# Making keys and queries behind the tiles of channels in a bidirectional encoder block: one phase's matmuls moved into another

## The chip, the cores and the metric

The kernel runs on one core of one Trainium2 chip. The metric is the device time of one execution in microseconds (us). The engines are PE (TensorE, matmuls), DVE (VectorE), ACT (ScalarE), POOL (GpSimd) and SP (SyncE), which issues most of the DMAs.

## The reference, cut

One layer of an encoder runs on a sample of 2048 rows and, with the same weights, on a prompt of 256 rows (`s` below); `D_MODEL` is 1024, there are 8 heads, a key has 64 plain and 32 rotary elements, a value has 64.

```python
def _layer(x, norm_pre, w_in, conv_w, q_norm, w_uq, kv_norm, w_ukv, w_out, norm_post):
    hdn = _rmsnorm(x, norm_pre)
    proj = jnp.einsum('bsd,de->bse', hdn, w_in)
    u, b_gate, c_gate, z_conv, q_lat, kv_lat, k_pe, z_attn = jnp.split(proj, _split_points(), axis=-1)
    conv_out = b_gate * _short_conv(c_gate * u, conv_w) * jax.nn.silu(z_conv)
    q = jnp.einsum('bsr,re->bse', _rmsnorm(q_lat, q_norm), w_uq).reshape(b, s, N_HEADS, QK_NOPE_DIM + QK_ROPE_DIM)
    q_nope, q_pe = jnp.split(q, [QK_NOPE_DIM], axis=-1)
    q_pe = _apply_rope(q_pe, cos[:, None, :], sin[:, None, :])
    kv = jnp.einsum('bsr,re->bse', _rmsnorm(kv_lat, kv_norm), w_ukv).reshape(b, s, N_HEADS, QK_NOPE_DIM + V_HEAD_DIM)
    k_nope, v = jnp.split(kv, [QK_NOPE_DIM], axis=-1)
    k_pe = _apply_rope(k_pe, cos, sin)
    ...
    attn_out = _attention(q_full, k_full, v) * jax.nn.silu(z_attn)
    mix = jnp.concatenate([conv_out, attn_out], axis=-1)
    out = jnp.einsum('bse,ed->bsd', mix, w_out)
    return x + _rmsnorm(out, norm_post)
```

## The kernel before, in words

The rows stand as T = 2304 columns, the sample's 2048 first and the prompt's 256 last. Every operand of a projection is kept as a high and a low part, and `mm3` (L87) multiplies high by high (L91), high by low (L92) and low by high (L93) into one PSUM tile: three matmuls for each term.

**Phase 1** (`phase1`, L103) goes over the rows in two halves `hf` of 1152. In each half it makes the latents of nine tiles of rows (`latents` L176, `turn_latents` L213: query latents of 384, key and value latents of 256 and the 32 rotary columns, stored to DRAM as `lat_s` and `kpe_s`), then goes through 20 tiles of 128 channels, `etile` (L242; 40 in both halves, counted by `n`). For each of three chunks `ci` of 384 rows `etile` issues 24 matmuls (8 terms) into a PSUM tile `o` of the tag `mm`, which has six buffers; DVE, ACT and POOL evacuate it as the kind of channel wants (`u`, gates, SiLU, and behind each fourth tile the short convolution `conv`, L295). The weights of a tile come through a staging buffer and are split into `whi` and `wlo` (`load_w`, L231). In the last four tiles of a half the chunks become the attention's gate `za`, which SP stores to `gate_s` (L256 to L258).

The opening of phase 2 is a generator, `Phase2.open` (L405). It loads the weights of the up-projections (uq, uk, uv) through two staging buffers, squares them (L436) for norms that scale them, sums these on PE (`w_ssq` L451, `rot_sum` L462, `all_sum` L484), turns the result into row scales, splits the weights into f16 high and low parts and rotates the key's 32 rotary columns into `kr_s`. `phase1` starts it behind tile 23 and takes two of its steps behind each tile from there.

**Phase 2** (`Phase2.run`, L559) works on nine chunks of 256 rows; chunk 0 is the prompt. `keys` (24 matmuls, a chunk's four tiles of 128 channels in one wide PSUM tile), `values` (12 matmuls of 512 columns in two halves) and `queries` (54 matmuls, two of six tiles rotary) come in the order k0 v0 q0, k1 v1 ... k8 v8, q1 ... q8. Keys and queries are evacuated chunk by chunk to f16 high and low parts and stored to DRAM (`kn_s`, `qn_s` on ACT's queue, `qr_s` on SP's). The attention loads them from there: `load_k` (five DMAs), `load_q_of` (nine DMAs), `load_kc` (two DMAs, the low parts of the rotary keys). For the prompt these are one `load_k` and two `load_q_of`; for the sample, `k_0` holds two heads over all 2048 rows and `q_0` two heads over 512.

Before a block's softmax the kernel takes the maximum of its scores: `max_chunks` (L733), for the prompt 8 steps `m_p`, for block 0 of the sample 32 steps `m_0`, each a matmul of 512 columns (L752) and a DVE reduction (L753). `max_columns` and `max_rows` (L756, L768) fold the maxima into the queries. `prompt` (L833) is the whole attention for a pair of the prompt's heads: scores `sp`, ACT's exponents `pp`, POOL's sum `accp`, the product with the values `op`, and `finish` (L811) with `rp` and the division. `tile_encoder` (L974) drives all that: it takes one step of a generator at a time behind each tile that `run` yields, the prompt's steps (`sides["p"]`) behind k3 and later, the rest of them at q1, and block 0's maxima (`sides[0]`) behind the query tiles q3 to q8. From the first key tile on PE, DVE, ACT and POOL run in the order in which the program says it (`manual_schedule`); in phase 1, and on SP throughout, the framework's scheduler sets the order.

Then follow the **attention** of the sample (`steps` L861, `values` L911, with the first product of weights and values at L920) and **phase 4**, the output projection. The change leaves both as they are.

Of the kernel before, what the change touches and what calls it, by code (L numbers as in the profile page):

```python
# [21 lines left out]
P = 128  # L22
# [80 lines left out]
def phase1(g, x, x_t, w_e, w_lat, npre, convw, open_phase2):  # L103

    nc, tc = g.nc, g.tc
    with ExitStack() as ctx:
# [135 lines left out]
        def etile(n):  # L242
# [3 lines left out]
            for ci in range(3):  # L246
# [84 lines left out]

        n = 0
        for hf in range(2):
# [24 lines left out]
            for j in range(5):  # L358
                if j < 4:
                    edge(hf, j, True)  # L360
                for e in range(4):
# [3 lines left out]
                    etile(n)  # L365
# [23 lines left out]
class Phase2:  # L389
# [15 lines left out]
    def open(self, w_uq, w_uk, w_uv, w_lat, npre, qg, kvg, pst, ps):  # L405
# [4 lines left out]

        g, nc, tc = self.g, self.g.nc, self.g.tc
# [30 lines left out]
        yield  # L442
# [15 lines left out]
        yield  # L458
# [22 lines left out]
        yield  # L481
# [16 lines left out]
        yield  # L498
# [9 lines left out]
        yield  # L508
        for m in range(0, 12, 3):
# [3 lines left out]
            if m % 2:  # L513
                yield

        for name, src, kt, n, at in srcs[1:] + srcs[:1]:
            hi, lo = self.ws[name]
            for k in range(kt):
# [4 lines left out]
                yield  # L523

        for a, b in ((0, 768), (768, 1536), (1536, TS), (TS, T)):
# [5 lines left out]
            yield  # L531
# [7 lines left out]
            yield  # L539
        for what in ("kv", "q"):  # L540
            self.load(0, pw, what)
        tmp.close()


    def load(self, ci, pb, what):

        g, nc = self.g, self.g.nc
        at, n = self.chunks[ci]
        a, num = (3, 2) if what == "kv" else (0, 3)
        lt = pb.tile([P, n // P, 2, num, P], F16, tag=f"lt_{what}", bufs=1 if ci == 0 else 4 if what == "kv" else 2, name=f"lt_{what}{ci}")  # L550
# [3 lines left out]
        if what == "q":  # L554
            tb = pb.tile([P, 2, CB], F32, tag="tb", bufs=1 if ci == 0 else 2, name=f"tb{ci}")
            nc.sync.dma_start(tb[:, :, :n], self.table[:, :, at % TS : at % TS + n])
        self.lt[what, ci] = lt, tb

    def run(self, pv):  # L559

        g, ws = self.g, self.ws
        nc, tc = g.nc, g.tc
        with ExitStack() as ctx:
            pb = ctx.enter_context(tc.tile_pool(name="p2b", bufs=2, reuse_waits="tile"))

            def rope(dst, src, tb, name):

                t = pb.tile([P, 2, CB], F32, tag="rs", bufs=2, name=f"rs_{name}")[:, :, : src.shape[2]]
                cos, sin = (tb[:, w : w + 1, : src.shape[2]].to_broadcast(list(src.shape)) for w in range(2))
                nc.vector.stream_shuffle(t, src, SWAP)  # L570
                nc.vector.tensor_tensor(dst, src, cos, op=ALU.mult)
                nc.gpsimd.tensor_tensor(t, t, sin, op=ALU.mult)
                nc.gpsimd.tensor_tensor(dst, dst, t, op=ALU.add)

            late = []

            def store(queue, dst, src, tok):

                queue.dma_start(dst[:, :, tok].rearrange("w (m p) t -> p w m t", p=P), src)

            def block(name, n):
                return pb.tile([P, 2 * 4 * CB], F16, tag="s4", bufs=3, name=name)[:, : 8 * n].rearrange("p (w m t) -> p w m t", w=2, m=4)

            def wide(name, m, n):
                return g.wide(name)[:, : m * n].rearrange("p (m t) -> p m t", m=m)

            def keys(ci):
                at, n = self.chunks[ci]
                lt, _ = self.lt["kv", ci]
                sk = block(f"sk{ci}", n)  # L590
                hi, lo = ws["uk"]
                o = wide(f"k{ci}", 4, n)
                for m in range(4):
                    msl = slice(m * P, (m + 1) * P)
                    mm3(nc, o[:, m], [(hi[:, k, msl], lo[:, k, msl], lt[:, :, 0, k], lt[:, :, 1, k]) for k in range(2)])
                    if m == 3:
                        split(nc, sk[:, 0], sk[:, 1], o, BACK)
                        late.append(lambda: store(nc.scalar, g.kn, sk, slice(at, at + n)))
                    yield "k", ci, m

            def values(ci):
                at, n = self.chunks[ci]
                lt, _ = self.lt["kv", ci]
                hi, lo = ws["uv"]
                o = wide(f"v{ci}", n // P, H * DV)
                for m in range(n // P):
                    mm3(nc, o[:, m], [(lt[:, m, 0, k], lt[:, m, 1, k], hi[:, k, :], lo[:, k, :]) for k in range(2)])
                    if m == n // P - 1:
                        nc.scalar.activation(pv[:, at // P : (at + n) // P], o, AF.Copy, scale=BACK)
                        while late:  # L610
                            late.pop(0)()
                    yield "v", ci, m

            def queries(ci):
                at, n = self.chunks[ci]
                tok = slice(at, at + n)
                lt, tb = self.lt["q", ci]
                sqr = pb.tile([P, 2, CB], F32, tag="sqr", bufs=1, name=f"sqr{ci}")[:, :, :n]
                sqp = pb.tile([P, 2, 2, CB], F16, tag="sqp", bufs=1, name=f"sqp{ci}")[:, :, :, :n]
                sq = block(f"sq{ci}", n)  # L620
                hi, lo = ws["uq"]
                r = g.narrow(f"qr{ci}", "o")[:, : 2 * n].rearrange("p (m t) -> p m t", m=2)
                o = wide(f"q{ci}", 4, n)
                for m in (4, 5, 0, 1, 2, 3):
                    msl = slice(m * P, (m + 1) * P)
                    mm3(nc, o[:, m] if m < 4 else r[:, m - 4], [(hi[:, k, msl], lo[:, k, msl], lt[:, :, 0, k], lt[:, :, 1, k]) for k in range(3)])
                    if m == 5:
                        rope(sqr, r, tb, f"q{ci}")
                    if m == 3:
                        split(nc, sq[:, 0], sq[:, 1], o, BACK)  # L630
                        nc.scalar.activation(sqp[:, 0], sqr, AF.Copy, scale=BACK)
                        nc.gpsimd.tensor_scalar(sqr, sqr, BACK, None, op0=ALU.mult)
                        nc.gpsimd.tensor_tensor(sqp[:, 1], sqr, sqp[:, 0], op=ALU.subtract)
                        store(nc.scalar, g.qn, sq, tok)
                        store(nc.sync, g.qr, sqp, tok)
                    yield "q", ci, m

            last = len(self.chunks)
            plan = [("kv", 0), ("q", 0)] + [("kv", ci) for ci in range(1, last)] + [("q", ci) for ci in range(1, last)]
            ahead = [(w, ci) for w, ci in plan if ci]  # L640
            for i, (what, ci) in enumerate(plan):
                while ahead and plan.index(ahead[0]) <= i + (3 if ahead[0][0] == "kv" else 1):
                    w, c = ahead.pop(0)
                    self.load(c, pb, w)
                if what == "kv":
                    yield from keys(ci)
                    yield from values(ci)
                else:
                    yield from queries(ci)
# [324 lines left out]
def tile_encoder(ctx, tc, x, x_t, w_e, w_lat, w_uq, w_uk, w_uv, w_out, convw, npre, qg, kvg, npost, table, y):  # L974
# [35 lines left out]
    side = []  # L1010

    def prompt():

# [9 lines left out]
    sides = {"p": prompt(), 0: at.max_chunks(0)}  # L1023
    last = len(p2.chunks) - 1
    for kind, ci, m in p2.run(g.v):
        if (kind, ci, m) == ("k", 0, 0):
            order.enter_context(tc.manual_schedule(engines=engines))
            at.load_kc()
        if (kind, ci, m) == ("q", 0, 3):
            at.load_k("p")  # L1030
            at.load_q("p")

            nc.scalar.activation(at.ps.tile([P, 10], F32, tag="warm", bufs=1, name="warm"), g.mhalf, AF.Exp)
        if (kind, ci, m) == ("v", last, 1):
            at.load_k(0)
        if (kind, ci, m) == ("q", 2, 3):
            at.load_q(0)
        if kind in "kv" and ci > 2:
            next(sides["p"], None)
        if (kind, ci, m) == ("q", 1, 4):  # L1040
            for _ in sides["p"]:
                pass
        if kind == "q" and (ci > 3 or ci == 3 and m in (2, 3)):
            next(sides[0], None)
        if (kind, ci, m) == ("q", 7, 3):
            at.load_q(1)
    for _ in sides[0]:
# [100 lines left out]
```

## Time and profile before

| | |
|---|---|
| Median of 3 runs | 1690.15 us (1689.59 to 1693.16) |
| Profiled execution, its own time | 1692.56 us |
| its span in the trace | 1690.6 us, mean granted clock 0.994 |
| PE busy | 1647.5 us (97%) |
| POOL, DVE, ACT busy | 878.5, 750.2, 581.6 us |
| Phase 1, tiles of channels, second half | 392.5 to 646.1 us of the span |
| Phase 2, prompt and block 0's maxima | 646.1 to 812.9 us |
| Attention of the sample | 812.9 to 1483.9 us |

A row of the timeline or of a group names the line, the operation, its output and inputs, the shape and the duration; what stands in brackets behind a row is the idle time of the engine just ahead of it and the work that ended this. PEclk is the share of TensorE's full clock that was granted in a stretch.

### The profile page before, as it was taken

How to read it: one execution, taken by the hardware profiler on the slowest of the kernel's cores; microseconds unless marked ns; L12 is line 12 of the kernel's file. 1: busy time of each engine (PE TensorE's matmuls, PEld its weight loads, DVE VectorE, ACT ScalarE, POOL GpSimd, SP SyncE). 2: the span in 40 equal slices, each digit the busy share in tenths (PEclk: the TensorE clock that was granted, in tenths of full speed). 3: DMA queues.
4: the chain of work that ended last, by engine and by line, in shares of the span. 5: the costliest groups of instructions: out<-in, count | busy, mean ns of one | idle time of the engine just before them, and what ended most of it. 6: DMA issues, size and time to landing. Idle time of an engine off the chain costs nothing. (4 is left out here: it accounts for less than half of the span.)

```text
span 1690.6 us, 22364 instructions
## 1 busy us (share of the span) xinstructions
PE 1647.5 (97%) x8870; PEld 1115.8 (66%) x8870; DVE 750.2 (44%) x1125; ACT 581.6 (34%) x804; POOL 878.5 (52%) x637
## 2 busy tenths in 40 slices
PE   8999999999999999978999999999999999999998
PEld 8999999999999997556333333333333333378886
DVE  4333332423474222337556665666666666132122
ACT  7521111452222122411444444444444444512211
POOL 3321221033342112145788988989899898942222
PEclk9999999999999999989999999999999999999999
DMA  8921112364324116378011131113111210034443
GB/s 292 273 87 60 52 52 83 112 165 118 114 94 137 55 62 167 106 194 214 13 32 32 44 85 41 44 32 94 31 45 32 69 44 13 26 105 144 149 141 109
DMA packets 141741, 158.97 MB, mean 94 GB/s; under 512 B 33842, under 2 KB 118116, under 8 KB 141636
## 3 DMA queue, kind: packets, MB, share of 16 engines
q1 hardware_dynamic: 122916, 148.11, 29.3%
q10 hardware_dynamic: 18720, 9.44, 1.9%
q8 instruction: 69, 1.13, 0.3%
q14 instruction: 36, 0.29, 0.1%
HBM read 109.72 MB, written 41.89 MB: 90 GB/s over the span
## 5 line engine op out<-in xcount | busy, mean ns | idle before, releaser
L809 POOL TENSOR_TENSOR acc<-acc,p 128x1024 f32<-128x1024 f32 x224 | 527.9, 2357 | 60.6 <-ACT p L799 50.5
L753 DVE TENSOR_REDUCE mx<-m 128x1 f32<-128x512 f32 x512 | 337.7, 691 | 237.2 <-PE m L752 237.1
L799 ACT ACTIVATE p<-s,exps 128x1024 f32<-128x1024 f32 x256 | 271.4, 1111 | 348.2 <-PE s L794 348.2
L91 PE MATMUL o<-hdn_hi,whi 128*128 128x384 f32 x960 | 323.5, 337 | 0.0
L92 PE MATMUL o<-hdn_lo,whi 128*128 128x384 f32 x960 | 322.7, 336 | 0.0
L93 PE MATMUL o<-hdn_hi,wlo 128*128 128x384 f32 x960 | 322.6, 336 | 0.0
L789 PE MATMUL s<-q,k 128*128 128x512 f16 x1024 | 302.7, 381 | 1.0 <-ACT p L799 1.0
L920 PE MATMUL o<-p,v 128*64 128x512 f32 x1024 | 247.7, 605 | 0.0
L789 PEld LDWEIGHTS <-k 128*128 128x128 f16 x1024 | 90.7, 98 | 190.8 <-issue 101.4
L752 PE MATMUL m<-k,q 96*128 96x512 f16 x512 | 195.4, 382 | 14.4 <-DVE mx L753 8.7
L91 PEld LDWEIGHTS o<-hdn_hi,whi 128*128 128x128 f32 x960 | 180.5, 188 | 0.5
L92 PEld LDWEIGHTS o<-hdn_lo,whi 128*128 128x128 f32 x960 | 180.5, 188 | 0.0
L93 PEld LDWEIGHTS o<-hdn_hi,wlo 128*128 128x128 f32 x960 | 180.5, 188 | 0.0
L920 PEld LDWEIGHTS o<-p,v 128*64 128x64 f32 x1024 | 62.2, 136 | 127.5 <-issue 127.0
L959 PE MATMUL out<-wo,o_cut 128*128 128x512 f32 x576 | 140.4, 396 | 0.0
L959 PEld LDWEIGHTS out<-wo,o_cut 128*128 128x128 f32 x576 | 108.0, 188 | 27.7 <-issue 0.8
L948 POOL TENSOR_TENSOR o_cut<-o_raw,o_cut 128x1024 fp32r<-128x1024 f32 x17 | 40.8, 2399 | 118.3 <-ACT o_cut L945 118.3
L279 POOL TENSOR_TENSOR gt<-gt,z 128x384 f32<-128x384 f32 x24 | 28.7, 1197 | 141.1 <-ACT z L278 141.1
L236 ACT ACTIVATE whi<-w 128x1024 fp32r<-128x1024 f32 x40 | 42.2, 1058 | 172.8 <-PE o L92 159.6
L752 PEld LDWEIGHTS <-q 96*128 96x128 f16 x512 | 49.6, 97 | 63.9 <-issue 6.2
L967 DVE TENSOR_TENSOR yt<-out,g_post 128x1024 f32<-128x1024 f32 x18 | 22.0, 1224 | 150.7 <-ACT junko L966 141.7
L271 POOL TENSOR_TENSOR cu<-cu,rb 128x384 f32<-128x384 f32 (+2 forms) x28 | 27.5, 987 | 112.4 <-DVE cu L270 112.4
(230 smaller groups left out, 2016.4 us busy)
## 6 DMA issues: line engine op xcount, KB each, us to landing
w<-in_w_e_dram SPq DMA_DIRECT2D x40, 512.0 KB, 3.5
x<-in_x_dram SPq DMA_DIRECT2D x18, 512.0 KB, 6.8
o_raw<-mix_s SPq DMA_DIRECT2D x18, 512.0 KB, 4.8
o_raw<-in_x_dram SPq DMA_DIRECT2D x18, 512.0 KB, 5.6
out_dram<-yt SPq DMA_DIRECT2D x18, 512.0 KB, 6.2
q<-qn_s SPq DMA_DIRECT2D x64, 128.0 KB, 2.7
xt<-in_x_t_dram SPq DMA_DIRECT2D x5, 1536.0 KB, 8.3
k<-kn_s SPq DMA_DIRECT2D x12, 512.0 KB, 7.1
```

What stands on the lines that cost most here:

```text
L91: nc.tensor.matmul(out, sh, mh, start=first and i == 0, stop=False)
L92: nc.tensor.matmul(out, sh, ml, start=False, stop=False)
L93: nc.tensor.matmul(out, sl, mh, start=False, stop=last and i == n - 1)
L236: nc.scalar.activation(hi, w, AF.Copy)
L752: nc.tensor.matmul(m, q[:DQK, i, 2, b * P : (b + 1) * P], k[:DQK, i, 1, c * 512 : (c + 1) * 512], start=True, stop=True)
L753: nc.vector.reduce_max(mx[:, u, c : c + 1], m, axis=AX.X)
L789: nc.tensor.matmul(o, k[:, ki, x, ks], q[:, qi, x, :], start=x == 0, stop=False)
L799: nc.scalar.activation(p, o, AF.Exp, scale=g.exps[:, 0:1])
L809: nc.gpsimd.tensor_tensor(self.acc[key], self.acc[key], first, op=ALU.add)
L920: nc.tensor.matmul(self.o[n][i * DV : (i + 1) * DV], g.v[:, kt, h * DV : (h + 1) * DV], p[:, i * QB : (i + 1) * QB], start=kt == 0, stop=k ...
L948: eng.tensor_tensor(ml, m, f(mh), op=ALU.subtract)
L959: nc.tensor.matmul(o[:, w], mh[:, k, :], wk[k // 2][:, k % 2, w], start=k == 0 and wk is hi, stop=False)
```

## The change

Keys and queries of all nine chunks move into phase 1. `etile` calls `between` behind each of its three chunks. `between` takes one step of the opening, and where that step yields 2, two more. The opening starts behind tile 21 instead of tile 23 (`n == 22`), its steps come one behind each chunk, and `keys_queries` follows as part of it: 90 tiles of keys and queries, three behind each of the last thirty chunks. Each has a PSUM tile of its own, of the tag `mm` that the chunks use, is evacuated by itself, and all stores go through SP. Phase 2 keeps the values alone; the prompt's attention and block 0's maxima are interleaved with their eighteen halves and with each other in a new way. The loads of keys and queries for the prompt stand right behind phase 1, those of block 0 behind the first two chunks of values. The number of PE's instructions stays 10976.

```diff
-        def etile(n):
+        def etile(n, between):
...
                     nc.sync.dma_start(g.gate[e * P : (e + 1) * P, c * CH : (c + 1) * CH], za)
+                    between()
                     continue
...
                     conv(hf, j, ci)
+                between()
...
+        opening = iter(())
+
+        def between():
+            for _ in range(next(opening, 0)):
+                next(opening, None)
...
-                    etile(n)
+                    etile(n, between)
...
-                    if n == 24:
+                    if n == 22:
                         opening = open_phase2(pb, ps)
-                    if n >= 24:
-                        next(opening, None)
-                        next(opening, None)
...
-        for what in ("kv", "q"):
-            self.load(0, pw, what)
         tmp.close()
+        self.pb = self.ctx.enter_context(tc.tile_pool(name="p2b", bufs=2, side="right", reuse_waits="tile"))
+        yield from self.keys_queries(ps)
+        for ci in range(3):
+            self.load(ci, "kv")
...
+    def keys_queries(self, ps):
...
+        last = len(self.chunks)
+        for ci in range(2):
+            self.load(ci, "kv")
+            self.load(ci, "q")
+        for ci, (at, n) in enumerate(self.chunks):
+            tok = slice(at, at + n)
+            for what, name, kt, ms in (("kv", "k", 2, 4), ("q", "q", 3, 6)):
...
+                for m in range(ms):
+                    msl = slice(m * P, (m + 1) * P)
+                    o = ps.tile([P, CH], F32, tag="mm", bufs=6, name=f"{name}{ci}_{m}")[:, :n]
+                    mm3(nc, o, [(hi[:, k, msl], lo[:, k, msl], lt[:, :, 0, k], lt[:, :, 1, k]) for k in range(kt)])
+                    if m < 4:
+                        split(nc, s[:, 0, m], s[:, 1, m], o, BACK)
+                    else:
+
+                        t, r = (pb.tile([P, CB], F32, tag=tag, name=f"{tag}{ci}_{m}") for tag in ("rs", "sqr"))
+                        nc.vector.stream_shuffle(t, o, SWAP)
+                        nc.vector.tensor_tensor(r, o, tb[:, 0], op=ALU.mult)
+                        nc.gpsimd.tensor_tensor(t, t, tb[:, 1], op=ALU.mult)
+                        nc.gpsimd.tensor_tensor(r, r, t, op=ALU.add)
+                        nc.scalar.activation(sp[:, 0, m - 4], r, AF.Copy, scale=BACK)
+                        nc.vector.scalar_tensor_tensor(sp[:, 1, m - 4], r, BACK, sp[:, 0, m - 4], op0=ALU.mult, op1=ALU.subtract)
+                    if m == 3:
+                        store(g.kn if what == "kv" else g.qn, s, tok)
+                    if m == 5:
+                        store(g.qr, sp, tok)
+                    if m == ms - 1 and ci + 2 < last:
+                        self.load(ci + 2, what)
+                    yield 2
...
+        for ci, (at, n) in enumerate(self.chunks):
+            if ci + 3 < last:
+                self.load(ci + 3, "kv")
...
+            for m in range(2):
+                mm3(nc, o[:, m], [(lt[:, m, 0, k], lt[:, m, 1, k], hi[:, k, :], lo[:, k, :]) for k in range(2)])
+                if m:
+                    nc.scalar.activation(pv[:, at // P : (at + n) // P], o, AF.Copy, scale=BACK)
+                yield ci, m
...
-    sides = {"p": prompt(), 0: at.max_chunks(0)}
...
+    order.enter_context(tc.manual_schedule(engines=engines))
+    at.load_k("p")
+    at.load_q("p")
+    at.load_kc()
+
+    nc.scalar.activation(at.ps.tile([P, 10], F32, tag="warm", bufs=1, name="warm"), g.mhalf, AF.Exp)
+    side = prompt()
+    for ci, m in p2.run(g.v):
+        if (ci, m) == (1, 0):
             at.load_k(0)
-        if (kind, ci, m) == ("q", 2, 3):
             at.load_q(0)
...
+            first = at.max_chunks(0)
+        if ci > 1:
+            next(side, None)
+        if ci > 2:
+            next(first, None)
+            if m:
+                next(side, None)
+    for _ in side:
+        next(first, None)
+        next(first, None)
+    at.load_q(1)
+    for _ in first:
         pass
     at.max_columns(0)
```

The next two pieces show **PE at the first maximum of block 0** (`m_0_0`). Before, it stands among the query tiles of chunk 3:

```order
L93 MATMUL q_6651<-lt_q_6556,uq_lo 128x256
L752 LDWEIGHTS q_6632
L752 MATMUL m_0_0_6703<-k_6474,q_6632 128x512
L91 LDWEIGHTS uq_hi
L91 MATMUL q_6651<-lt_q_6556,uq_hi 128x256
```

With the change it stands behind the third of the prompt's maxima and ahead of the second half of the values of chunk 3:

```order
L719 MATMUL m_p_7077<-k_p,q_p_6964 128x256
L729 LDWEIGHTS q_7024
L729 MATMUL m_0_0_7082<-k_7018,q_7024 128x512
L91 LDWEIGHTS lt_kv_6991
L91 MATMUL v_7070<-uv_hi,lt_kv_6991 128x512
```

So PE reaches its first use of `k_0` and `q_0` after three and a half of nine chunks of values; before, all values and three chunks of queries stood ahead of it. On **SP behind phase 1** the DMAs of `k_0` (`k_6474` before, `k_7018` now) stood among those of the query chunks:

```order
L729 DMA gate_7574<-gate_s 128x512
L556 DMA tb_6559<-in_table_dram 128x2x256
L693 DMA k_6474<-kn_s 64x2x2048
L696 DMA k_6474<-kn_s 64x2x2048
L697 DMA k_6474<-kn_s 64x2x2048
L579 DMA qr_s<-sqp_6486 128x4x256
L552 DMA lt_q_6556<-lat_s 128x2x384 x2
```

Now they stand behind all eighteen DMAs of the prompt's queries, the two of `kc` and two latent loads:

```order
L700 DMA q_p_6974<-qr_s 32x2x256 x2
L660 DMA kc<-kr_s 32x2304 x2
L562 DMA lt_kv_7008<-lat_s 128x2x256 x2
L670 DMA k_7018<-kn_s 64x2x2048
L671 DMA k_7018<-kr_s 32x2x2048
L672 DMA k_7018<-kr_s 32x2x2048
L673 DMA k_7018<-kn_s 64x2x2048
L674 DMA k_7018<-kn_s 64x2x2048
L691 DMA q_7024<-qn_s 64x2x512
L692 DMA q_7024<-qr_s 32x2x512
```

The nine loads of `q_0` follow those of `k_0` with nothing between them. The third place is the **opening on PE**. The sums of the squared weights, `w_ssq`, stood behind the last chunk of tile 23 and `rot_sum` three chunks later:

```order
L92 MATMUL o_2_3915<-hdn_lo_3078,whi_3757 128x384
L93 MATMUL o_2_3915<-hdn_hi_3077,wlo_3758 128x384
L451 LDWEIGHTS uq_sq
L451 MATMUL w_ssq<-short,uq_sq 128x2
L451 LDWEIGHTS uq_sq
```

Now `w_ssq` stands behind the second chunk of tile 22, and `rot_sum` behind the third:

```order
L92 MATMUL o_1_3842<-hdn_lo_2833,whi_3662 128x384
L93 MATMUL o_1_3842<-hdn_hi_2832,wlo_3663 128x384
L458 LDWEIGHTS uq_sq
L458 MATMUL w_ssq<-short,uq_sq 128x2
L458 LDWEIGHTS uq_sq
```

```order
L91 MATMUL o_2_3908<-hdn_hi_3077,whi_3662 128x384
L92 MATMUL o_2_3908<-hdn_lo_3078,whi_3662 128x384
L93 MATMUL o_2_3908<-hdn_hi_3077,wlo_3663 128x384
L469 MATMUL rot_sum<-rot,ones 128x2
L91 MATMUL o_0_3966<-hdn_hi_2414,whi_3757 128x384
```

So the sums come four chunks earlier on PE, and only one chunk lies between the squares' sums and the next step that needs them. The key and query tiles themselves stand on PE from the second chunk of tile 29 on, three tiles behind each chunk; a chunk's matmuls load their weights themselves, those of the f16 tiles have an instruction for it ahead of each.

## Rows read from the trace of the kernel before

**Rows 1.** Windows: us, busy (x) of PE, PEld, DVE, ACT, POOL, PEclk, DMA share, GB/s.

```profile
392.53:646.14 253.61, 252.22 (x1486) 250.94 (x1484) 107.37 (x200) 54.39 (x89) 72.89 (x80) 1.00 0.30 96
646.14:722.59 76.45, 71.91 (x506) 45.24 (x506) 27.89 (x36) 29.75 (x38) 13.18 (x12) 1.00 0.56 152
722.59:798.80 76.21, 59.61 (x466) 46.68 (x465) 38.47 (x62) 12.07 (x16) 38.58 (x30) 0.91 0.83 212
812.91:1483.87 670.96, 667.62 (x3204) 224.44 (x3203) 388.02 (x578) 306.36 (x317) 602.23 (x274) 1.00 0.15 43
```

**Rows 2.** Timeline of PE among the query tiles: start, length, instruction [idle before].

```profile
740.79 0.37 PE L91 MATMUL qr<-lt_q,uq_hi 128*128 128x256 f16 x1 [6.24 <-DMA lt_q<-lat_s]
752.56 0.58 PE L752 MATMUL m<-k,q 96*128 96x512 f16 x1 [5.12 <-DMA q<-qr_s]
```

**Rows 3.** Windows of PE alone: a key chunk's 24 matmuls, a query chunk's.

```profile
646.14:648.75 2.61, 2.61 (x24) 1.00 0.42 127
722.59:728.49 5.90, 5.90 (x56) 1.00 0.36 110
```

**Rows 4.** Timeline of PE in phase 1, from a small matmul to the latents' fp32r ones.

```profile
377.50 0.43 PE L91 MATMUL pq<-wl_hi,hdn_hi 128*128 128x384 f32 x1
377.76 0.34 PE L92 MATMUL pq<-wl_lo,hdn_hi 128*128 128x384 f32 x1
```

**Rows 5.** Timelines of PE, SP and DVE in the opening.

```profile
442.78 0.28 PE L451 MATMUL w_ssq<-short,uq_sq 128*128 128x2 bf16 x5
...
419.90 0.33 SPq L227 DMA_DIRECT2D kpe_s<-kpt  x1
434.38 0.80 SPq L435 DMA_DIRECT2D uks<-in_w_uk_dram  x2
...
447.68 0.16 DVE L456 TENSOR_TENSOR rot<-ssq 128x1 fp32r<-128x1 f32 x1
```

**Rows 6.** Timeline of SP's queue behind phase 1.

```profile
646.67 0.33 SPq L258 DMA_DIRECT2D gate_s<-za  x1
664.96 0.59 SPq L714 DMA_DIRECT2D q_p<-qn_s  x1
675.22 0.90 SPq L723 DMA_DIRECT2D q_p<-qr_s  x2
727.62 0.59 SPq L693 DMA_DIRECT2D k<-kn_s  x1
750.10 0.54 SPq L715 DMA_DIRECT2D q<-qr_s  x1
```

**Rows 7.** Window in which `k_0`'s large loads move, columns as in rows 1.

```profile
733.00:736.00 3.00, 1.55 (x15) 1.14 (x12) 1.05 (x2) 1.02 (x1) 2.54 (x3) 1.00 1.02 219
```

**Rows 8.** The prompt: window of its `mrp` matmuls, and timeline of one pair of heads.

```profile
680.55:682.80 2.25, 1.21 (x18) 1.09 (x16) 1.18 (x1) 1.76 (x5) 0.00 (x0) 1.00 0.89 258
...
708.73 0.27 PE L845 MATMUL sp<-q_p,k_p 128*128 128x256 f16 x1
710.65 0.28 PE L794 MATMUL sp<-q_p,kc 33*128 33x256 f16 x1
712.13 1.08 PE L857 MATMUL op<-pp,v 128*64 128x256 f32 x8 [0.44 <-ACT pp L799]
713.54 0.65 PE L818 MATMUL rp<-accp,ones_f 128*64 128x256 f32 x4 [0.33 <-POOL accp L851]
```

**Rows 9.** Timelines of DVE and PE from the last maxima to the first values.

```profile
801.99 3.09 DVE L753 TENSOR_REDUCE mx<-m 128x1 f32<-128x512 f32 x5
804.53 0.38 PE L776 MATMUL mr<-ident,mst 128*97 128x128 f16 x4 [0.24 <-DVE mx L753]
812.91 0.65 PE L920 MATMUL o<-p,v 128*64 128x512 f32 x2
```

**Rows 10.** Groups by line: DVE's reciprocals of the prompt.

```profile
L823 DVE RECIPROCAL rsump<-rsump 128x128 f32<-128x128 f32 x8 | 7.0, 922 | 10.9 <-ACT rsump L820 10.9
```

**Rows 11.** Waits: engine, line, waited for; us in total, times, longest us.

```profile
ACT cy L309 <- POOL cu L271: 64.6, 16, 7.1
```

More of the change, by code (lines that the diff above doesn't have):

```diff
@@ L441, in open @@
         nc.scalar.activation(wt, wt, AF.Square, accum_out=kp)
-        yield
+        yield 0
         acc = ps.tile([P, 3, P], F32, tag="tl", name="w_ssq")[:, 0, :28]
@@ L480, in open @@
         unpower(nc, g.inv, col)
-        yield
+        yield 0
         acc = ps.tile([P, 3, P], F32, tag="tl", name="all_sum")[:, 0, :2]
@@ L507, in open @@
             nc.vector.tensor_scalar(diag[:, m], g.ident, c, W_UP, op0=ALU.mult, op1=ALU.mult)
-        yield
+        yield 0
         for m in range(0, 12, 3):
@@ L513, in open @@
             if m % 2:
-                yield
+                yield 0
         for name, src, kt, n, at in srcs[1:] + srcs[:1]:
@@ L538, in open, with load @@
             nc.sync.dma_start(g.kr[:, :, a:b].rearrange("w e t -> e w t"), krp)
-            yield
-        for what in ("kv", "q"):
-            self.load(0, pw, what)
+            yield 0
         tmp.close()
-    def load(self, ci, pb, what):
-        g, nc = self.g, self.g.nc
+        self.pb = self.ctx.enter_context(tc.tile_pool(name="p2b", bufs=2, side="right", reuse_waits="tile"))
+        yield from self.keys_queries(ps)
+        for ci in range(3):
+            self.load(ci, "kv")
+    def load(self, ci, what):
+        g, nc, pb = self.g, self.g.nc, self.pb
         at, n = self.chunks[ci]
         a, num = (3, 2) if what == "kv" else (0, 3)
-        lt = pb.tile([P, n // P, 2, num, P], F16, tag=f"lt_{what}", bufs=1 if ci == 0 else 4 if what == "kv" else 2, name=f"lt_{what}{ci}")
+        turn = self.turn = self.turn + 1
+        lt = pb.tile([P, n // P, 2, num, P], F16, tag=f"lt_{what}", bufs=4 if what == "kv" else 2, name=f"lt_{what}{turn}")
         for w in range(2):
@@ L554, in load @@
         if what == "q":
-            tb = pb.tile([P, 2, CB], F32, tag="tb", bufs=1 if ci == 0 else 2, name=f"tb{ci}")
+            tb = pb.tile([P, 2, CB], F32, tag="tb", name=f"tb{ci}")
             nc.sync.dma_start(tb[:, :, :n], self.table[:, :, at % TS : at % TS + n])
         self.lt[what, ci] = lt, tb
-    def run(self, pv):
[L561 to L649, printed above, removed]
@@ new lines, in keys_queries, with store @@
+    def keys_queries(self, ps):
+        g, ws, nc, pb = self.g, self.ws, self.g.nc, self.pb
+        def store(dst, src, tok):
+            nc.sync.dma_start(dst[:, :, tok].rearrange("w (m p) t -> p w m t", p=P), src)
+        last = len(self.chunks)
[5 more added lines that the diff above has]
+            for what, name, kt, ms in (("kv", "k", 2, 4), ("q", "q", 3, 6)):
+                lt, tb = self.lt.pop((what, ci))
+                hi, lo = ws["u" + name]
+                s = pb.tile([P, 2, 4, CB], F16, tag="s4", bufs=3, name=f"s{name}{ci}")
+                if what == "q":
+                    sp = pb.tile([P, 2, 2, CB], F16, tag="sqp", name=f"sqp{ci}")
+                for m in range(ms):
[19 more added lines that the diff above has]
+                    yield 2
@@ new lines, in run @@
+    def run(self, pv):
+        g, nc = self.g, self.g.nc
+        hi, lo = self.ws["uv"]
+        last = len(self.chunks)
+        for ci, (at, n) in enumerate(self.chunks):
+            if ci + 3 < last:
+                self.load(ci + 3, "kv")
+            lt, _ = self.lt.pop(("kv", ci))
+            o = g.wide(f"v{ci}").rearrange("p (m e) -> p m e", m=2)
+            for m in range(2):
[3 more added lines that the diff above has]
+                yield ci, m
@@ L1021, in prompt @@
             yield from at.prompt(j)
-    sides = {"p": prompt(), 0: at.max_chunks(0)}
[L1024 to L1034, printed above, removed]
+    order.enter_context(tc.manual_schedule(engines=engines))
[6 more added lines that the diff above has]
+        if (ci, m) == (1, 0):
             at.load_k(0)
-        if (kind, ci, m) == ("q", 2, 3):
             at.load_q(0)
[L1038 to L1047, printed above, removed]
+            first = at.max_chunks(0)
[10 more added lines that the diff above has]
+    for _ in first:
         pass
```

9 lines of the change are left out of this document (4 added, 5 removed).

## The prediction

> **What bounds the kernel now.** I read the stages first, as windows: by what is PE held in each? In the second half of phase 1 and in the sample's attention PE is busy for 252 of 254 us and 668 of 671 [rows 1]; no cover is wanted there, and work added there costs its full length. Only the stretch between them has slack: 646.1 to 722.6 and 722.6 to 798.8, where PE is busy 71.9 and 59.6 us, the second at a granted clock of 0.91, and on to the first product with the values at 812.9 [rows 1, 9]. Then the timeline of that stretch: the reader should see two waits for a DMA, 6.24 us for a latent load of the queries and 5.12 us for `q_0` [rows 2]. The change takes key and query matmuls out of this stretch and puts them where PE never waits. The question is whether the stretch shrinks by as much as phase 1 grows. So I forecast two instants: E, where phase 1 ends and the values begin (646.1 before), and the start of the sample's values on PE (812.9 before). Behind that nothing changes and PE sets the pace, so the shift of 812.9 is the shift of the whole.
>
> **E: phase 1 grows.** A key chunk's 24 matmuls take 2.61 us, a query chunk's 54 take 5.90 (its window holds 56 entries) [rows 3]. Nine of each are 9 x 8.51 = 76.6 us, at the same pace as before, since they stand in program order between chunks that never wait. There are 30 changes from f16 to the chunks' matmuls. The nearest rows are a small matmul's successor in phase 1: its second matmul starts 0.26 us after it, against 252.2 / 1486 = 0.17 in the long run [rows 4, 1]; 0.07 to 0.09 for each makes 2 us (0 if the load of weights is covered, 4.5 if both directions cost that and more). The matmuls of the tiles stay hidden for evacuation as long as six PSUM buffers bridge it: the 90 tiles add splits on ACT and DVE, which are busy 54 and 107 of 254 us there [rows 1], so I cost them at nothing. That cover is gone where one of them stands behind an instruction that waits, such as ACT's `cy`, which waits for POOL up to 7.1 us [rows 11]; that is a rival below.
>
> By the Trainium skill ("TensorE: Matmul & The Clock Gate", part on LDWEIGHTS) PE pulls weight loads ahead of matmuls in flight, so the changes of type would cost nothing and the sum would be 2 us less; the row with 0.26 us speaks for a small price.
>
> The opening starts two tiles earlier, and its sums are packed closer. On PE `w_ssq` stood behind tile 23; four chunks of 24 matmuls, 4.1 us each at 0.17, are 16.4 us, so it is reached at 442.8 - 16.4 = 426.4 [rows 5]. But the squares are made from loads on SP, and these stand behind the store of `kpe_s` at 419.9, whose work doesn't move. The second weights' load (`uks`) can follow at about 422 when its buffer is free, instead of at 434.4; from it to DVE's `rot` it took 447.7 + 0.2 - 434.4 = 13.5 us [rows 5], so `rot` is there at 435.5. PE, with one chunk between, wants `rot_sum` at 426.4 + 4.1 = 430.5: a stall of 5 us (none if the loads run ahead of what I think, 6 if the loads are slower). E = 646.1 + 76.6 + 2 + 5 = 729.7.
>
> **R: when block 0's first maximum can start.** On PE the first maximum now stands after three and a half chunks of values and three maxima of the prompt: about 3.5 x 2.6 (a value chunk has as many columns as a key chunk, 2.61 [rows 3]) plus 1, or E + 10. It needs `k_0` and `q_0`. On SP these stand behind the last gate store, at E + 0.5 [rows 6], then k_p (5 DMAs), q_p (18), kc (2), a latent load (2). SP issues q_p's eighteen from 664.96 to 676.12, 11.2 us or 0.62 each [rows 6]. So k_p is out at E + 3.2 and q_p at E + 14; k_0's first DMA starts at E + 15.7, its five take 3.1, and the first two DMAs of q_0, all that a maximum reads, are out at E + 20.1. From the issue of such a one (750.10) to the matmul that waited for it (752.56) were 2.5 us [rows 6, 2]: R = E + 22.5 if DMAs flow freely. They don't: in the stretch where k_0's large pieces moved the DMA engines were fully used at 219 GB/s [rows 7]; k_0 is 512 KB three times and 256 KB twice, 2.1 MB, 10 us at that rate, and q_0 queues behind it. From E + 15.7 + some 1.5 to land that gives R = E + 27 (bounds 22.5 and 31, the latter if q_p, still moving, delays it). PE waits for 17 us at the first maximum, and because PE runs in order, all the rest of the prompt's attention waits behind it: what was a queue of short waits becomes one long one.
>
> By the Trainium skill ("DMA: Bandwidth & Descriptors", measured bandwidth) 1 MB moves in 6.15 us; k_0 would take some 6 us, R would be about E + 23.5 and the sum 3.5 us less; the row of 219 GB/s in this kernel speaks against it.
>
> **From R to the first values of the sample.** What follows R on PE, in program order:
> - Five halves of values, the rest of the prompt's maxima and six of block 0's: 6.5 + 2.4 us, with 3 for a slower clock after the wait and for DVE: 12.
> - The prompt's column maxima 2.25 [rows 8], and its first pair of heads: scores 708.7 to 710.9, 2.1 us, then exponents and POOL's sum until `rp` is through at 714.2, 3.3 us [rows 8]. 7.6 in sum; the chains of ACT and POOL are no longer covered by key matmuls, as they were at 710.9 to 712.1.
> - Three halves and three maxima 4.5, second pair 5.4: 9.9. Two halves and two maxima 3.0, third pair 5.4: 8.4.
> - The tail, paced by DVE: of 32 maxima 18 or so are left, each 0.62 (five in 3.09 [rows 9]), 11.2; with them the reciprocals, four of 0.92 [rows 10], and two divisions and waits for the last pair 2.5: 17.4.
>
> Sum 55.5 us. From the last maximum PE still has the columns and rows of block 0 and two steps of scores: on DVE five reductions of 0.62 are still to go, 3.1, and with the fold of the columns 4.4 (an estimate), and `mr` to the first values 812.91 - 804.53 = 8.4 [rows 9], together 12.8.
>
> **The sum.** 729.7 + 27 + 55.5 + 12.8 = 825.0, against 812.9: 12.1 us later. The profiled execution took 1692.56 with a span of 1690.6; it would take 1704.7. The median of the runs is 2.4 below that execution, so 1690.15 + 12.1 gives **1702**.
>
> **Rivals.**
> 1. *Faster: the loads don't hold PE.* If k_0 and q_0 land by E + 10, PE never waits there; 17 us go and the result is 1685. It decides at R = E + 10 + 12 = E + 22: below that the change gains. For it: the DMA engines have room in phase 1, and a scheduler might issue what is ready earlier. Against: k_0 stands behind 27 DMAs in SP's order, at 0.62 each, and none of them can go ahead of the last stores of phase 1. Also in this case the prompt's chains may be better covered than I priced them. 0.16.
> 2. *No change.* R at the issue's bound (E + 22.5), and the opening hidden, takes 4.5 + 5 + 2 off: about 1690.6. For it: the squares' loads may be quick, as DMA was only 30% used there [rows 1]. 0.13.
> 3. *Slower still.* In phase 1 the tile evacuations queue behind waiting instructions of the short convolution [rows 11], the six PSUM buffers run out and PE waits in many of 30 groups; 0.3 us each is 9 us: 1711, with R at its late bound 1715. For it: DVE, ACT and POOL each get about three instructions more in each group. Against: they are busy well under half of that stretch [rows 1]. 0.15.
> 4. That the change doesn't do what it says: the order on PE shows the tiles in their new places and the same 10976 instructions; I give it no chance of its own.
>
> **How the numbers follow.** The forecast has 0.56, and nearly all of it is slower by over 0.2% (3.4 us, about what a measurement of this kernel can tell from no change): 0.54, and 0.02 same. With rival 3, slower is 0.69; with rival 2, same 0.15; rival 1 is faster 0.16. The range: the forecast's own is R from E + 22.5 to E + 31 and the opening from 0 to 6, some -8 and +5, or 1694 to 1707. It reaches down to 1688, which takes in rival 2 and the weak end of rival 1 and leaves out some 0.1, and up to 1714, leaving out the far end of rival 3, below 0.1.
>
> **What would show it.** Right: values start near 730 in the span; one wait of PE of 12 to 20 us at the first maximum of block 0, put down to a DMA into `q` or `k`; `w_ssq` or `rot_sum` with a few us of wait near 430; PE's clock lowered behind the long wait; waits of 1 to 2 us at `op` and `rp`; the first values of the sample near 825. Wrong: no wait over 5 us at that maximum (rival 1 or 2), E beyond 738 with many short waits at PSUM tiles of phase 1 (rival 3), or a shift behind 825 that differs from that at 825.

## The result, and the profile after

The changed kernel takes 1708.12 us (median of 4, 1705.92 to 1709.79); the kernel before, run beside it, 1691.66. The ratio is 1.0093, 95% interval 1.0076 to 1.011: slower by 0.9%, as forecast in sign, 6 us more than the 1702 forecast, inside the range. (1.5 of these 6 us lie in the kernel before, whose median here is not the 1690.15 that the forecast started from.) The profiled execution took 1709.41 us with a span of 1707.6, 17.0 more than the span before.

First the stages, as windows of the changed kernel with the columns of [rows 1]: phase 1 from where the old one ended, the values and the prompt, and a stretch of the sample's attention as long as the one shown of before.

```profile
646.14:728.41 82.27, 81.62 (x567) 76.84 (x566) 29.99 (x74) 20.39 (x48) 20.74 (x25) 1.00 0.41 125
728.41:829.63 101.22, 70.83 (x310) 27.63 (x309) 40.77 (x67) 23.65 (x33) 10.31 (x9) 0.78 0.52 127
829.63:1500.59 670.96, 667.62 (x3204) 224.49 (x3202) 387.64 (x577) 306.35 (x317) 602.27 (x274) 1.00 0.15 43
```

Phase 1 grew by 82.3 us, and in that stretch PE never waits for long. In the sample's attention PE, ACT and POOL are busy as before, to a few hundredths of a microsecond [rows 1]. The stretch between was 166.8 us (646.14 to 812.91) and is 101.2: it gave back 65.5 of the 82.3 us. The missing 16.7 us lie in there, where PE is now busy for 71 of 101 us at a clock of 0.78.

The timeline of PE gives the instants of the forecast: the first values, the first maxima of the prompt and of block 0, the first product with the values of the sample. Columns as in [rows 2].

```profile
728.41 0.38 PE L91 MATMUL v<-uv_hi,lt_kv 128*128 128x512 f16 x1 [0.65 <-DVE za L256]
...
736.48 0.38 PE L719 MATMUL m_p<-k_p,q_p 96*128 96x256 f16 x2 [1.44 <-DMA q_p<-qn_s]
...
757.73 0.58 PE L729 MATMUL m<-k,q 96*128 96x512 f16 x1 [17.84 <-DMA q<-qr_s]
758.11 0.63 PE L91 MATMUL v<-uv_hi,lt_kv 128*128 128x512 f16 x1
...
829.63 0.65 PE L897 MATMUL o<-p,v 128*64 128x512 f32 x2
```

The waits of 6.24 and 5.12 us for DMAs [rows 2] are gone, and one of 17.84 has come: the first maximum waits for `q_0`. Behind it a value matmul that took 0.38 us takes 0.63, at half the clock. What PE waited for, SP had issued in this order (timeline of SP's queue):

```profile
728.99 0.34 SPq L258 DMA_DIRECT2D gate_s<-za  x1
...
731.78 0.57 SPq L691 DMA_DIRECT2D q_p<-qn_s  x1
...
744.53 0.58 SPq L670 DMA_DIRECT2D k<-kn_s  x1
...
748.18 0.59 SPq L692 DMA_DIRECT2D q<-qr_s  x1
```

`k_0` begins 15.5 us behind the last gate store. The DMA that released PE was issued at 748.18 and PE went on at 757.73, 9.5 us later, against 2.5 for the same load before [rows 6, 2]. The window of PE's wait behind the first issue of `k_0` shows DMA engines with no room left, and a granted clock of 0.50:

```profile
744.53:757.73 13.20, 0.00 (x1) 0.03 (x1) 0.00 (x0) 0.00 (x0) 0.00 (x0) 0.50 0.99 225
```

### The profile page after: what moved, and what is told of

Its sections match the earlier page's. It is cut to its first block, busy times and chain, and to the rows that moved or that the text cites. A ratio compares the mean times of both kernels' runs of the same rounds, so it can differ in the third digit from the quotient of the medians.

```text
span 1707.6 us, 22569 instructions
## 1 busy us (share of the span) xinstructions
PE 1656.4 (97%) x8870; PEld 1115.1 (65%) x8870; DVE 759.4 (44%) x1224; ACT 590.4 (35%) x867; POOL 857.3 (50%) x637
## 5 line engine op out<-in xcount | busy, mean ns | idle before, releaser
L729 PE MATMUL m<-k,q 96*128 96x512 f16 x512 | 197.9, 387 | 24.6 <-DMA q<-qr_s 17.8
```

The source lines that it names most:

```text
L729: nc.tensor.matmul(m, q[:DQK, i, 2, b * P : (b + 1) * P], k[:DQK, i, 1, c * 512 : (c + 1) * 512], start=True, stop=True)
```

## The experiments

Two theories. **T1, the loads:** the long wait, and through it the slower clock, costs its length, and it is there because `k_0` and `q_0` stand behind 27 DMAs. **T2, the chains:** the stretch is paced by DVE's 40 maxima and by the prompt's way over ACT and POOL, and a wait taken out comes back further on. A summary first; E, the wait for the loads at block 0's first maximum and the sample's first product are from each kernel's timeline and waits.

| kernel | median us | ratio to before, 95% | E | wait at maximum | first product |
|---|---|---|---|---|---|
| before | 1689.6 to 1691.7 | | 646.1 | 5.1 | 812.9 |
| changed | 1708.12 | 1.0076 to 1.011 | 728.4 | 17.8 | 829.6 |
| e1 loads in order of need | 1690.54 | 0.9988 to 1.002 | 727.1 | 1.5 | 811.9 |
| e2 late maxima | 1714.17 | 1.0124 to 1.0154 | 728.5 | none (13.2 at values) | 834.9 |
| e3 gap in the opening | 1710.20 | 1.0108 to 1.0156 | 727.4 | 17.8 | 828.5 |
| e4 e1 and e3 | 1688.91 | 0.9981 to 1.0004 | 727.6 | 1.9 | 809.1 |
| e5 e1 and a spread order | 1678.72 | 0.9921 to 0.9954 | 728.6 | none | 798.8 |
| e6 e5 and a later opening | 1676.29 | 0.9907 to 0.9936 | 724.9 | none | 796.7 |
| e7 buffers of e1 alone | 1707.73 | 1.0082 to 1.0113 | 727.7 | 17.5 | 828.1 |
| e8 e7 and a spread order | 1696.68 | 1.0023 to 1.0047 | 727.0 | 15.1 | 817.3 |
| e9 e7 and late maxima | 1697.45 | 1.0024 to 1.005 | 728.1 | 3.2 | 818.1 |

**e1, the loads in order of need.** `load_k` and `load_q_of` become generators that stop behind the parts that maxima read; those of all four tiles are issued first, the rest behind the first chunks of values.

```diff
         nc.sync.dma_start(t[:NOPE, :, 1], hi)
         nc.sync.dma_start(t[NOPE:DQK, :, 1], rot)
+        yield
...
         nc.sync.dma_start(v[NOPE:DQK, :, 2], rot[0])
+        yield
...
+    loads = [at.load_k("p"), at.load_q("p"), at.load_k(0), at.load_q(0)]
+    for part in loads:
+        next(part)
     at.load_kc()
...
+        if (ci, m) in ((0, 0), (1, 0)):
+            for part in loads[2 * ci : 2 * ci + 2]:
+                for _ in part:
+                    pass
...
-        lt = pb.tile([P, n // P, 2, num, P], F16, tag=f"lt_{what}", bufs=4 if what == "kv" else 2, name=f"lt_{what}{turn}")
+        lt = pb.tile([P, n // P, 2, num, P], F16, tag=f"lt_{what}", bufs=8 if what == "kv" else 2, name=f"lt_{what}{turn}")
```

> Two theories of the 17 us that the change loses. T1, the loads: PE waits 17.8 us at the first maximum of block 0 because its keys and queries stand behind 27 other DMAs, and in a queue of megabytes; the wait costs its length and some slow clock behind it. T2, the chains: the stretch behind phase 1 is paced by DVE's 40 maxima and the prompt's chains over ACT and POOL, and a wait that goes there comes back further on. This kernel issues first the parts of the prompt's and block 0's keys and queries that the maxima read (8 DMAs, 1.7 MB, about 8 us at 219 GB/s), and the rest behind; the latents of the values get 8 buffers in place of 4, so that they stand ahead. T1: the wait at the first maximum is under 4 us, the first values of the sample come 14 to 17 us earlier (829.6 to about 814), 1691 to 1695. T2: the wait goes, but waits on DVE and ACT grow by nearly as much, 1702 or more.

1690.54 us, 17.6 less than the change, and the first product comes 17.7 us earlier. The wait is 1.51 us (timeline of PE):

```profile
738.54 0.38 PE L736 MATMUL m<-k,q 96*128 96x512 f16 x1 [1.51 <-DMA q<-qr_s]
738.76 0.38 PE L91 MATMUL v<-uv_hi,lt_kv 128*128 128x512 f16 x1
```

The value matmul behind it stays at full clock. From E to the first product e1 takes 84.8 us against 101.2, 16.4 less, and the wait is 16.3 shorter. T1 holds for nearly all of the loss, and T2 as a theory of it falls. Its timeline of SP shows the parts that the maxima read, ten DMAs and not the eight of the expectation, issued by 734.1 (three of k_p's parts and all of q_p's rest behind them):

```profile
724.02 0.63 SPq L670 DMA_DIRECT2D k_p<-kn_s  x1
...
731.59 0.58 SPq L670 DMA_DIRECT2D k<-kn_s  x1
...
733.48 0.59 SPq L699 DMA_DIRECT2D q<-qr_s  x1
```

But the end of the stretch is no shorter: windows from behind `rp` of the third pair of heads to the first product, of the changed kernel and of e1, each with a row of the sample's scores in it (timeline of PE).

```profile
797.68:829.63 31.95, 25.31 (x86) 7.76 (x84) 21.47 (x36) 5.28 (x8) 5.06 (x4) 0.68 0.50 115
...
826.54 0.59 PE L766 MATMUL s<-q,k 128*128 128x512 f16 x2
```

```profile
776.58:811.94 35.36, 27.31 (x87) 8.61 (x85) 21.63 (x36) 5.28 (x8) 5.05 (x4) 0.66 0.45 104
...
806.93 1.06 PE L773 MATMUL s<-q,k 128*128 128x512 f16 x2
```

In both PE runs at two thirds of its clock while DVE works off the maxima that are left, and in e1 the low clock lasts into these scores: here 3.4 us came back, which the wait for `q_p` (1.4 us, now gone) and the full clock behind the first maximum made up for. So T2 names a second cost, beside the first and not in its place.

**e2, the maxima later.** The loads stay; only PE's order changes.

```diff
-        if ci > 2:
+        if ci > 5:
             next(first, None)
+        if ci > 2:
             if m:
                 next(side, None)
```

> Only the order of PE is changed: block 0's maxima begin behind the values of chunk 6 in place of chunk 3, the loads stay. T1: PE has some 9 us more to do before it needs k_0 and q_0, the wait falls from 17.8 to about 9 us; six maxima more are left for the tail at 0.65 each, 4 us; net 4 to 6 us less, about 1703. T2: the tail takes back all of it, 1708 or more.

1714.17 us, 6 more than the change: the expectation fails, in size and sign. The waits of PE say where (engine, line, waited for, us in total, times, longest):

```profile
PE v L91 <- DMA lt_kv<-lat_s: 13.2, 2, 8.1
PE m L729 <- DVE mx L730: 6.1, 13, 1.0
PE mrp L753 <- ACT q_p L759: 1.8, 2, 1.4
```

The wait at the maximum is gone, and PE waits 13.2 us for latents of the values, which stand on SP behind `k_0` and `q_0`. The order of the loads catches PE at the next instruction that reads one. These waits are 4.6 us less than the one that went, but PE is busy for 79.1 us in place of 70.8 with the same matmuls, at a lower clock (the window stands in the last section). As this doesn't tell T1 from T2 cleanly, e9 repeats it with the latents ahead.

**e7, the control.** e1 had eight buffers for the latents; here they stand alone.

```diff
-        lt = pb.tile([P, n // P, 2, num, P], F16, tag=f"lt_{what}", bufs=4 if what == "kv" else 2, name=f"lt_{what}{turn}")
+        lt = pb.tile([P, n // P, 2, num, P], F16, tag=f"lt_{what}", bufs=8 if what == "kv" else 2, name=f"lt_{what}{turn}")
...
-        for ci in range(3):
+        for ci in range(7):
             self.load(ci, "kv")
...
-            if ci + 3 < last:
-                self.load(ci + 3, "kv")
+            if ci + 7 < last:
+                self.load(ci + 7, "kv")
```

> The changed kernel with eight buffers for the latents of the values in place of four, and nothing else: the control for the run with the loads in order of need, which had them too. T1: the wait at the first maximum stays (16 to 18 us), for the queue ahead of k_0 is the same but for some 2 latent loads; 1705 to 1709. If the buffers were what helped, it falls by over 5 us, under 1703.

1707.73 us: nothing that these runs can tell (0.4 us). Of e1's 17.6 us the other 17.2 are the order of the loads.

**e9, the maxima later, with the buffers of e7.** The diffs of e2 and e7 together.

> Eight buffers, and block 0's maxima begin behind the values of chunk 6, the loads in the change's order: the run with late maxima alone let PE wait 13.2 us for latents of the values that stood behind k_0 and q_0 in the queue. T1: with the latents ahead of them the wait at the maximum is 4 to 9 us in place of 17.8; three maxima more in DVE's tail cost 2 to 4 us of it; 1700 to 1705. If the length is set by the chains behind (T2), 1707 or more.

1697.45 us, less than expected. Three waits of PE in e9:

```profile
PE m L729 <- DVE mx L730: 6.1, 13, 1.0
PE m L729 <- DMA q<-qn_s: 3.2, 1, 3.2
PE mrp L753 <- ACT q_p L759: 1.8, 2, 1.4
```

The wait falls by 14.3 us against e7 and the time by 10.3: DVE's tail takes some of it back, 1.4 us in waits on DVE among it. So 10.3 us of the same loss can be mended from PE's side, without touching the loads' order, if nothing that PE needs earlier stands behind them.

**e3, a gap in the opening.** Two empty steps between the squares of the weights and their sums.

```diff
         nc.scalar.activation(wt, wt, AF.Square, accum_out=kp)
         yield 0
+        yield 0
+        yield 0
```

> Two empty steps of the opening between the squares of the weights and their sums, so that each later step comes two chunks (8.4 us) later, the keys and queries too (they still end in phase 1). T1: the waits at w_ssq (2.4 and 0.6 us) and the slow clock near 430 go, phase 1 ends 3 to 5 us earlier, about 1704. Rival: the stall only moves (the weights' loads or the splits come later too), 1707 to 1709.

1710.20 us: nothing is gained, as the rival said. Waits of PE in the changed kernel's opening, and in that of e3:

```profile
PE w_ssq L458 <- ACT uv_sq L443: 2.4, 2, 2.1
PE w_ssq L458 <- ACT uk_sq L443: 0.6, 1, 0.6
PE all_sum L491 <- DVE tot L482: 0.3, 1, 0.3
```

```profile
PE all_sum L493 <- DVE tot L484: 2.4, 1, 2.4
```

The stall left the squares' sums and came to a later one, `all_sum`. The steps from `rot_sum` to `tot`, which it waits for, are a chain over DVE and POOL; it took 4.5 us in the changed kernel, hardly more than a chunk, and 6.7 in e3, where steps of the short convolution (`cy`) stand among it on DVE. So a gap ahead of the chain moved the wait and didn't take it out.

**e4, e1 and e3 together.**

> The loads in order of need and the two empty steps together. T1: the gains add, 18 to 21 us less, 1687 to 1690, a little faster than the kernel before (1691.7). T2: 1698 or more, only the opening's gain.

1688.91 us, inside the expectation but not for its reason: the opening gained nothing, as in e3, and E stands at 727.6 against e1's 727.1. It is 1.6 under e1, whose runs go from 1686.2 to 1698.5, and its interval holds no change against the kernel before.

**e5, a spread order.** On e1; the loop now steps by a table, one entry for each half of values: p is a step of the prompt, m a maximum of block 0.

```diff
+    ORDER = ['', '', '', '', 'pp', 'pp', 'pp', 'pp', 'pmmm', 'pmmm', 'pmmm', 'mmm', 'mm', 'mmp', 'mmppmpmpp', 'mmppmpmpp', 'mmppmpmpp', 'mmppmpmp', 'mm']
...
-        if ci > 1:
-            next(side, None)
-        if ci > 2:
-            next(first, None)
-            if m:
-                next(side, None)
-    for _ in side:
-        next(first, None)
-        next(first, None)
+        step(ORDER[half])
+    step(ORDER[18])
```

The generator of the prompt has one more stop, behind its column and row maxima.

> The loads in order of need, and another order on PE, DVE and ACT behind phase 1: two of the prompt's maxima behind each of the fifth to eighth halves of values, up to three of block 0's behind each of the next six, then for each pair of the prompt's heads its scores, a half of values, two maxima, its products, two maxima. In the run with the loads in order alone the maxima left over for the end let PE wait for DVE, at half the clock from 780 to 800. T1 with this tail as its second part: DVE has 41 us of work in these 82 us and PE 54, so that a spread order takes 62 to 70 us from the first values to the sample's in place of 84.8: 1690.5 less 14 to 20, 1671 to 1676. T2, the chains set the pace: the prompt's four chains each still cost their length, and the time is over 1684.

1678.72 us: 11.8 less than e1, short of what was expected (14 to 20), and faster than the kernel before. Windows from the first values to the first product, in e1 and in e5:

```profile
727.14:811.94 84.80, 70.49 (x311) 27.80 (x310) 40.86 (x67) 23.63 (x33) 10.30 (x9) 0.84 0.59 139
```

```profile
728.55:798.76 70.21, 62.37 (x310) 26.76 (x309) 40.39 (x67) 23.63 (x33) 10.30 (x9) 0.93 0.71 168
```

DVE, ACT and POOL do the same work to half a microsecond in 14.6 us less. PE is busy for 8.1 us less with the same matmuls, at a clock of 0.93 in place of 0.84, and idle for 6.5 us less.

**e8, the spread order with the change's loads.** e7 and the table of e5.

> Eight buffers and the spread order on PE, DVE and ACT, but the loads in the change's order. T1: the first maximum of block 0 stands some 12 us behind the start of the values and k_0 and q_0 are there at 29, so a wait of 14 to 18 us comes back; the spread order saves its 8 to 14 us as it did with the loads in order; 1691 to 1698. If order alone were enough (T2), it is as fast as with the loads in order, 1678 to 1682.

1696.68 us, as expected, with this wait of PE:

```profile
PE m L729 <- DMA q<-qn_s: 15.1, 1, 15.1
```

With e7, e1 and e5 this closes the square: order of loads 17.2 us under the change's order on PE (e7 to e1) and 18.0 under the spread one (e8 to e5); order on PE 11.0 (e7 to e8) and 11.8 (e1 to e5). The two costs are separate and add, to within what such runs can tell (some 3 us for e1).

**e6, a later opening.** On e5; the opening starts behind tile 23 as before, and each step of `keys_queries` yields 3, so that four tiles stand behind a chunk.

```diff
-                    if n == 22:
+                    if n == 24:
...
-                    yield 2
+                    yield 3
```

> The same, the opening again from tile 24 on as in the kernel before, and four key or query tiles behind a chunk in place of three, so that they still end in phase 1. The stall at the sums of the weights was put down to the opening's early start: the loads of the weights stand on SP behind stores that don't come earlier. If so, PE waits under 1.5 us in the opening and phase 1 ends 2 to 4 us earlier (727.1 to about 724), if four tiles a chunk are still evacuated in time; the time is 2 to 4 us under the other run's. If the stall comes from the steps being one chunk apart, it stays, and the two are within 1 us.

1676.29 us, 2.4 less than e5, with E 3.7 us earlier and the first product 2.0. PE's waits in the opening fall from 3.0 us in e5 to 1.4: the early start made most of the stall. The steps are one chunk apart as before, so that isn't its main cause. What is left among the waits of PE:

```profile
PE w_ssq L458 <- ACT uv_sq L443: 0.7, 2, 0.5
PE rot_sum L469 <- DVE rot L464: 0.7, 1, 0.7
```

Four tiles a chunk are evacuated in time: PE waits for nothing else until the last of them. e6 beats both kernels: 0.9922 of the one before (0.9907 to 0.9936), 32 us under the change.

## Why the prediction was right, step by step

The mechanism was the one forecast: one long wait for `k_0` and `q_0`, in place of the slack that the key and query matmuls had filled. The forecast put the first product at 825.0; it came at 829.6. E was forecast 1.3 us too late, which hid a part of the other two errors, 2.3 and 3.6 us too little. Its instants:

- **E: 729.7 forecast, 728.4 measured.** Phase 1 grew by 82.3, of which some 5 went in the opening and 77 to the matmuls, forecast as 76.6. In the opening the forecast had `uks` issued at 422, PE at `w_ssq` at 426.4 and `rot` ready at 435.5. Timelines of SP, DVE and PE:

```profile
422.28 2.54 SPq L442 DMA_DIRECT2D uks<-in_w_uk_dram  x2
...
432.19 0.16 DVE L463 TENSOR_TENSOR rot<-ssq 128x1 fp32r<-128x1 f32 x1
...
435.12 0.14 DVE L464 TENSOR_SCALAR rot<-kp_ssq 128x1 fp32r<-128x1 f32 x1
...
426.52 0.60 PE L458 MATMUL w_ssq<-short,uq_sq 128*128 128x2 bf16 x18
...
436.58 0.17 PE L469 MATMUL rot_sum<-rot,ones 128*128 128x2 f32 x1
```

  The loss was of the forecast's size, but not in its place. I had charged 5 us at `rot_sum`; PE came to it at 436.58, 1.3 us after `rot` was there, and didn't wait. It had lost its time at `w_ssq`: 3.0 us in waits for ACT's squares (the rows under e3) and about 2 in the clock, 0.89 in the mean from 426.5 to 442. Without a stall `w_ssq` (0.9 us in the kernel before) and a chunk of 4.1 would have brought it to `rot_sum` at 431.5. The cause that I named, loads of the weights that stand late on SP, was right: ACT waited for `uvs`. The row that I timed for `rot` [rows 5] was that of its other half (here L463), which came 10 us behind `uks` and not 13.5. That the loss came to 5 us all the same is in part luck.

  The 2 us for changes of type were too much. Timeline of PE at one group of query tiles between two chunks:

```profile
708.98 0.34 PE L93 MATMUL o<-hdn_hi,wlo 128*128 128x384 f32 x1
709.16 0.28 PE L91 MATMUL q<-lt_q,uq_hi 128*128 128x256 f16 x1
...
712.01 0.27 PE L93 MATMUL q<-lt_q,uq_lo 128*128 128x256 f16 x1
712.04 0.42 PE L91 MATMUL o<-hdn_hi,whi 128*128 128x384 f32 x1
712.30 0.34 PE L92 MATMUL o<-hdn_lo,whi 128*128 128x384 f32 x1
```

  The 0.26 us behind the chunk's first matmul, which I read as its price [rows 4], is there; but that matmul starts only 0.03 us after the last f16 one, in place of 0.11. The two cancel: 0.08 saved, 0.09 lost, some 0.01 a group. I had read one interval of a pair. "TensorE: Matmul & The Clock Gate" of the Trainium skill (part on LDWEIGHTS, loads pulled ahead of matmuls in flight) has the next weights load while a matmul runs. These rows, with some 0.01 us lost a group, agree with it.
- **R: E + 27 forecast, E + 29.3 measured.** The issue was right (`k_0` at E + 15.7 forecast, E + 16.1 measured). The term that was too small is the transfer, 11.3 us against 13.2: at 225 GB/s, 13.2 us move 3.0 MB. I had counted `k_0`'s 2.1 MB, not what of the prompt's loads and of `q_0`'s other parts moves beside it. The table in "DMA: Bandwidth & Descriptors" of the Trainium skill (measured bandwidth) has 6.15 us and 341 GB/s for 1 MB. I took the rate, which put R at E + 23.5; by the time, the 2.1 MB of `k_0` take 12.9 us and R is E + 30.1, both estimates. With the DMA engines 0.99 busy this kernel moved 225 GB/s, and the measurement decides. From E to the first issue of `k_0` the engines had room, as this window shows:

```profile
728.41:744.53 16.12, 10.04 (x48) 4.51 (x47) 2.15 (x4) 5.09 (x6) 0.00 (x0) 0.92 0.69 173
```

  So the first 16 of the 29.3 us were paced by SP's issue of the loads ahead, and the last 13 by bytes. e1 cuts both at once; no run tells what each is worth, and none issues a part of the loads from another engine.
- **From R to the first product: 68.3 forecast, 71.9 measured.** (The forecast's pieces add to 55.3, not 55.5.) By these pieces, from the starts on PE: 12.0 forecast and 12.2 measured to `mrp`; 7.6 and 8.3 for the first pair; 9.9 and 10.5; 8.4 and 9.0; the tail 17.4 and 20.0; the columns and first steps 12.8 and 11.9. Each pair of heads was 0.6 or 0.7 short. The tail was mis-sized most. I took DVE's pace, 0.62 for each maximum, for the whole of it; window of the tail, and timeline of DVE in it:

```profile
797.68:817.69 20.01, 15.43 (x44) 3.95 (x43) 13.80 (x23) 1.88 (x3) 2.71 (x3) 0.56 0.37 84
...
807.95 1.29 DVE L730 TENSOR_REDUCE mx<-m 128x1 f32<-128x512 f32 x2 [3.04 <-PE m L729]
...
811.98 1.29 DVE L730 TENSOR_REDUCE mx<-m 128x1 f32<-128x512 f32 x2 [2.74 <-PE m L729]
```

  DVE is busy for 13.8 of the 20.0 us. It stands idle for 3.0 and 2.7 us while PE makes the scores of the last pair, and then its products, with only two maxima between them. PE's clock falls while it waits for DVE, to 0.56 in the mean of this window, so that these scores take 3.5 us in place of 2.1. The two take turns, and the forecast had them side by side.
- **The rivals.** That the loads don't hold PE (rival 1) was wrong by its own mark, R at or before E + 22: it was E + 29.3. The mark itself was misworked: the forecast's sum breaks even with R 12.1 us earlier, at E + 14.9, and e1, with R at E + 11.4, has the first product 1.0 us ahead of the kernel before. Rival 3's evacuations didn't stall phase 1: from 646.1 to 728.4 PE is busy for 81.6 of 82.3 us, and from 392.5 to 646.1 its only waits are the 3.3 us at the sums of the weights. Behind 829.6 the shift stays: 16.7 us there, 17.0 at the end.

## What to carry to other kernels

When work is moved out of a stretch with slack, ask what that work was covering. Here key and query matmuls hid most of the loads of the attention's first operands (5.1 us of wait showed); without them the loads' order in the queue became PE's order of waiting. Put first in a queue the part of each operand that is read first, and count bytes as well as issues. An engine that runs in order stops at the first late operand with everything behind it, so see for each operand both when it lands and what PE has to do until then.

## What the hardware showed that I had not expected

A wait costs more than its length: in the wait for `q_0` the granted clock went to 0.50 of full, the level of 1.2 GHz, and the next value matmul took 0.63 us in place of 0.38. Short waits cost clock too: in e1, where PE's longest wait from E to the first product is 1.5 us, PE is busy for 70.5 us at a mean clock of 0.84, and in e5 for 62.4 at 0.93, with the same matmuls. In e2, whose two waits for latents are of 5.1 and 8.1 us, it is busy for 79.1 at 0.76 (window from the first values to the first product):

```profile
728.50:834.93 106.43, 79.06 (x310) 29.23 (x309) 40.74 (x67) 23.62 (x33) 10.30 (x9) 0.76 0.50 121
```

The mean clock of a stretch alone doesn't give that time: the changed kernel is busy for only 70.8 us at 0.78, as a part of its low clock fell into the long wait, in which PE had nothing to do.
